# Softmax over 4096 rows of 32768: every second tile loaded in two transfers, the last tile cut finer

## The chip, the cores and the metric

The kernel runs on one core of a Trainium2 chip. The metric is the device time of one execution in microseconds: the median of three runs. A profile of one further execution, with the trace of every instruction and DMA packet, stands beside it. Five engines matter here. VectorE (DVE) takes maxima and scales, ScalarE (ACT) takes exponentials and scales, and SyncE (SP) issues transfers; ACT issues transfers too. The transfers themselves run on 16 DMA engines.

## The reference

```python
batch, seq, vocab = 16, 256, 32768
logits = np.random.randn(batch, seq, vocab).astype(np.float32)   # temperature = 1.0

scaled = logits / temperature
scaled = scaled - scaled.max(axis=-1, keepdims=True)
exp_scaled = np.exp(scaled)
return (exp_scaled / exp_scaled.sum(axis=-1, keepdims=True)).astype(np.float32)
```

A softmax over the last axis, in float32: 4096 rows of 32768 elements, 536.87 MB read and 536.87 MB written.

## The kernel before

Each row is split in two halves (`_SPLIT = 2`), so that the work is 8192 half rows of `W` = 16384 elements, 64 KB each. A tile is 128 half rows, one per partition; there are `G` = 64 tiles, and a tile's buffer takes 64 KB per partition. There are three buffers (`_BUFS = 3`), `x0` to `x2` (the trace calls all of them `x`); tile `t` uses buffer `t % 3`, is loaded into it, normalised in place and stored from it. The order of the instructions is written out by hand (`tc.manual_schedule()`); waits between engines and transfers are put in by the framework.

`normalise(t)` cuts the tile into pieces along the free axis, 4096, 4096, 4096, 2048 and 2048 elements in most tiles (`_PIECES`). It works as follows.

- For each piece, DVE takes the negated maximum `nm` of the piece (L101), and ACT replaces the piece by the exponential with that maximum as its bias, summing it into `ssum` (L108). Each piece so has its own maximum.
- The least of the negated maxima, `nMh`, is taken over the pieces (L119) and over the two halves of a row, by a shuffle between neighbouring partitions (`combine`, L77 and L80). ACT takes `ee`, the correction of each piece (L121).
- DVE sums the corrected sums (L124), combines the halves, takes the reciprocal `rS` (L135) and the final factor `f` of each piece (L136).
- Each piece is multiplied by its factor. Part of it is scaled by DVE (L140), the rest by ACT (L144); `_ON_DVE` = (4096, 4096, 2048, 0, 0) says how many elements of each piece go to DVE.

The first and the last tile, 0 and 63, are cut into four pieces of 4096 (`_END`), with 2560 elements of each on DVE (`_END_ON_DVE`). They are also loaded in four transfers of 16 KB per partition each, where other tiles are loaded in one transfer of 64 KB per partition (`_LOAD`), that is 8.39 MB. The last tile is stored piece by piece as pieces are scaled; the others in one transfer.

All loads are issued from SP (L62). Stores are issued from ACT (L70), those of the last two tiles from SP. The order is: loads of tiles 0, 1 and 2, and then for each tile `normalise(t)` and the load of tile `t + 2`, which waits until the store of tile `t - 1`, in the same buffer, has landed:

```python
for t in range(_BUFS):
    load(t)
for t in range(G):
    normalise(t)
    if t and t + _BUFS - 1 < G:
        load(t + _BUFS - 1)
```

In the trace, the load queue of SP is q1 and the store queue of ACT is q10; a transfer becomes packets of one row of one partition, so that a load of 64 KB per partition is 128 packets, eight on each DMA engine, and a four-byte completion packet on each.

Of the kernel before, what the change touches and what calls it, by code (L numbers as in the profile page):

```python
# [1 line left out]

# [4 lines left out]


_SPLIT = 2
_BUFS = 3  # L10
_LOAD = 16384
_PIECES = (4096, 4096, 4096, 2048, 2048)
_ON_DVE = (4096, 4096, 2048, 0, 0)
_END = 4096
_END_ON_DVE = 2560
_SETS = 3


@with_exitstack
def kernel(  # L20
    ctx: ExitStack,
    tc: tile.TileContext,
    logits: bass.AP,
    temperature: bass.AP,
    out: bass.AP,
):
    nc = tc.nc
    inv_t = 1.0 / float(temperature)
    P = nc.NUM_PARTITIONS
    fp32 = mybir.dt.float32  # L30
    Exp = mybir.ActivationFunctionType.Exp
    Copy = mybir.ActivationFunctionType.Copy
    X = mybir.AxisListType.X
    A = mybir.AluOpType

    xf = logits.flatten_outer_dims()
    of = out.flatten_outer_dims()
    N, V = xf.shape
    W = V // _SPLIT
    assert sum(_PIECES) == W and len(_PIECES) == len(_ON_DVE)  # L40
    x = xf.rearrange("n (h v) -> (n h) v", h=_SPLIT)
    o = of.rearrange("n (h v) -> (n h) v", h=_SPLIT)
    G = N * _SPLIT // P
    assert G * P == N * _SPLIT
    n_rounds = _SPLIT.bit_length() - 1
    K = max(len(_PIECES), W // _END)

    pool = ctx.enter_context(tc.tile_pool(name="fixed", bufs=1))
    buf = [pool.tile([P, W], fp32, tag=f"x{b}", name=f"x{b}") for b in range(_BUFS)]
    widths = dict(nm=K, ssum=K, ee=K, f=K, ttj=K, nMh=2, Sh=2, rS=1)  # L50
    stat = [
        {
            k: pool.tile([P, w], fp32, tag=f"{k}{s}", name=f"{k}{s}")
            for k, w in widths.items()
        }
        for s in range(_SETS)
    ]

    def load(t: int) -> None:
        n = _END if t in (0, G - 1) else _LOAD  # L60
        for s in range(0, W, n):
            nc.sync.dma_start(  # L62
                out=buf[t % _BUFS][:, s : s + n],
                in_=x[t * P : (t + 1) * P, s : s + n],
            )

    def store(t: int, a: int, b: int) -> None:

        engine = nc.sync if t >= G - 2 else nc.scalar
        engine.dma_start(  # L70
            out=o[t * P : (t + 1) * P, a:b], in_=buf[t % _BUFS][:, a:b]
        )

    def combine(v, op) -> None:
        for j in range(n_rounds):
            mask = [i ^ (1 << j) for i in range(32)]
            nc.vector.stream_shuffle(  # L77
                out=v[:, j + 1 : j + 2], in_=v[:, j : j + 1], mask=mask
            )
            nc.vector.tensor_tensor(  # L80
                out=v[:, j + 1 : j + 2],
                in0=v[:, j : j + 1],
                in1=v[:, j + 1 : j + 2],
                op=op,
            )

    def normalise(t: int) -> None:
        xs = buf[t % _BUFS]
        if t in (0, G - 1):
            sizes = [_END] * (W // _END)  # L90
            on_dve = [_END_ON_DVE] * len(sizes)
        else:
            sizes, on_dve = _PIECES, _ON_DVE
        K = len(sizes)
        at = [sum(sizes[:k]) for k in range(K)]
        st = stat[t % _SETS]
        nm, ssum, ee, f, ttj = (st[k][:, :K] for k in ("nm", "ssum", "ee", "f", "ttj"))
        nMh, Sh, rS = st["nMh"], st["Sh"], st["rS"]
        for k in range(K):
            xc = xs[:, at[k] : at[k] + sizes[k]]  # L100
            nc.vector.tensor_reduce(  # L101
                out=nm[:, k : k + 1], in_=xc, axis=X, op=A.max, negate=True
            )
            if inv_t != 1.0:
                nc.vector.tensor_scalar_mul(
                    out=nm[:, k : k + 1], in0=nm[:, k : k + 1], scalar1=inv_t
                )
            nc.scalar.activation(  # L108
                out=xc,
                in_=xc,  # L110
                func=Exp,
                bias=nm[:, k : k + 1],
                scale=inv_t,
                accum_out=ssum[:, k : k + 1],
            )
            if t == 1 and k == 0:

                store(0, 0, W)
        nc.vector.tensor_reduce(out=nMh[:, 0:1], in_=nm, axis=X, op=A.min)  # L119
        combine(nMh, A.min)  # L120
        nc.scalar.activation(  # L121
            out=ee, in_=nm, func=Exp, bias=nMh[:, n_rounds : n_rounds + 1], scale=-1.0
        )
        nc.vector.tensor_tensor_reduce(  # L124
            out=ttj,
            in0=ee,
            in1=ssum,
            scale=1.0,
            scalar=0.0,
            op0=A.mult,  # L130
            op1=A.add,
            accum_out=Sh[:, 0:1],
        )
        combine(Sh, A.add)
        nc.vector.reciprocal(out=rS, in_=Sh[:, n_rounds : n_rounds + 1])  # L135
        nc.vector.tensor_scalar_mul(out=f, in0=ee, scalar1=rS)  # L136
        for k in range(K):
            a, b, c = at[k], at[k] + on_dve[k], at[k] + sizes[k]
            if b > a:
                nc.vector.tensor_scalar_mul(  # L140
                    out=xs[:, a:b], in0=xs[:, a:b], scalar1=f[:, k : k + 1]
                )
            if c > b:
                nc.scalar.activation(  # L144
                    out=xs[:, b:c], in_=xs[:, b:c], func=Copy, scale=f[:, k : k + 1]
                )
            if t == G - 1:
                store(t, a, c)
        if 0 < t < G - 1:
            store(t, 0, W)  # L150

    with tc.manual_schedule():
# [8 lines that stand above are left out]
# [1 line left out]
_INS = ['logits', 'temperature']  # L162
_OUTS = [((16, 256, 32768), 'float32')]

_NUMBERS = {'temperature': 1.0}


# [26 lines left out]
```

## Time and profile before

| what | value |
|---|---|
| time, median of 3 | 2494.04 us (2493.56 to 2495.87) |
| span of the profiled execution | 2496.7 us |
| DVE busy | 1575.6 us, 63% |
| ACT busy | 1367.8 us, 55% |
| read and written | 536.87 MB each, 430 GB/s over the span |
| DVE waiting for loads (L101) | 683.8 us in 66 waits |
| ACT waiting for maxima (L108) | 1025.3 us |
| maximum of 4096 / 2048 elements, DVE | 4.413 / 2.276 us each |
| exponential of 4096 / 2048 elements, ACT | 3.708 / 1.985 us each |
| issue of a load on SP | 0.328 us (median) |

The times of DVE and ACT are sums over the whole run; what they waited for is named by the instruction that was held up. A DMA share of 1.00 in a stretch means that all 16 engines had packets in hand for all of it; values of 1.01 or a little more come from packets that began in the stretch and ended after it.

### The profile page before, as it was taken

To read this page: it belongs to the slowest core of one execution; us is meant where nothing else is said; L and a number is where in the kernel's file an instruction comes from. 1 tells how busy PE (TensorE), PEld (TensorE's weight loads), DVE (VectorE), ACT (ScalarE), POOL (GpSimd) and SP (SyncE) were. 2 spreads that over 40 slices of the span, in tenths; PEclk is the share of its full clock that TensorE was granted. 3 is DMA by queue.
4 is the path that set the end of the run, shared out by engine and by line. 5 is a ranking of instruction groups with operands and counts; after the bars stand their busy time and mean duration, and the time that the engine had idled before them with its cause. 6 is when DMAs were issued, how large, how long until landed. Compare 5 with 4: busy or idle time off the path is not lost.

```text
span 2496.7 us, 2616 instructions
## 1 busy us (share of the span) xinstructions
DVE 1575.6 (63%) x1216; ACT 1367.8 (55%) x895; POOL 0.2 (0%) x4
## 2 busy tenths in 40 slices
DVE  6576665766657656576565665656657566565665
ACT  6464654645546455464554645546455464554655
POOL 0000000000000000000000000000000000000000
DMA  9999999999999999999999999999999999999998
GB/s 419 436 429 430 433 437 436 435 437 426 434 434 437 433 426 435 434 436 423 433 433 433 435 425 436 436 433 425 435 422 436 421 437 436 421 436 422 436 429 380
DMA packets 19748, 1073.91 MB, mean 430 GB/s; under 512 B 2192, under 2 KB 2192, under 8 KB 2192
## 3 DMA queue, kind: packets, MB, share of 16 engines
q1 hardware_dynamic: 10800, 553.65, 51.4%
q10 hardware_dynamic: 8928, 520.10, 48.4%
q14 instruction: 20, 0.16, 0.0%
HBM read 536.87 MB, written 536.87 MB: 430 GB/s over the span
## 4 chain that ended last, share of the span: by engine, by line
DMA 73%; DVE 16%; ACT 9%; another core or an unknown queue 2%; issue 0%; SPq 0%; DVEq 0%; ACTq 0%
DMA x<-in_logits_dram 37%; DMA out_dram<-x 36%; DVE nm L101 12%; ACT x L108 7%; DVE x L140 3%; ACT x L144 2%; DVE f L136 0%; ACT ee L121 0%; DVE rS L135 0%; DVE Sh L80 0%; DVE ttj L124 0%; DVE Sh L77 0%; SPq L62 0%; DVEq L189 0%
## 5 line engine op out<-in xcount | busy, mean ns | idle before, releaser
L101 DVE TENSOR_REDUCE nm<-x 128x1 f32<-128x4096 f32 x318 | 1117.5, 3579 | 683.8 <-DMA x<-in_logits_dram 683.8
L108 ACT ACTIVATE x<-x,nm 128x4096 f32<-128x4096 f32 x318 | 965.4, 3036 | 1025.3 <-DVE nm L101 1025.3
L144 ACT ACTIVATE x<-x,f 128x2048 f32<-128x2048 f32 (+1 forms) x194 | 370.9, 1975 | 74.0 <-DVE f L136 74.0
L140 DVE TENSOR_SCALAR x<-x,f 128x4096 f32<-128x4096 f32 (+2 forms) x194 | 372.2, 1975 | 2.5 <-DVE f L136 0.2
L124 DVE CUSTOM_DVE_ANT_0 ttj<-ee,ssum 128x5 f32<-128x5 f32 (+1 forms) x64 | 10.6, 166 | 196.7 <-ACT ee L121 196.7
L108 ACT ACTIVATION_READ_ACCUMULATOR x<-x,nm 128x1 f32 x318 | 59.2, 186 | 0.0
L121 ACT ACTIVATE ee<-nm,nMh 128x5 f32<-128x5 f32 (+1 forms) x64 | 18.1, 284 | 0.0
L136 DVE TENSOR_SCALAR f<-ee,rS 128x5 f32<-128x5 f32 (+1 forms) x64 | 14.8, 231 | 2.2
L135 DVE RECIPROCAL rS<-Sh 128x1 f32<-128x1 f32 x64 | 10.5, 164 | 2.2
L80 DVE TENSOR_TENSOR Sh<-Sh 128x1 f32<-128x1 f32 x64 | 10.2, 159 | 2.2
L80 DVE TENSOR_TENSOR nMh<-nMh 128x1 f32<-128x1 f32 x64 | 10.2, 159 | 2.2
L119 DVE TENSOR_REDUCE nMh<-nm 128x1 f32<-128x5 f32 (+1 forms) x64 | 10.1, 158 | 2.2
L77 DVE STREAM_SHUFFLE Sh<-Sh 128x1 f32<-128x1 f32 x64 | 9.7, 151 | 0.0
L77 DVE STREAM_SHUFFLE nMh<-nMh 128x1 f32<-128x1 f32 x64 | 9.7, 151 | 0.0
L108 ACT ACT_TABLE_LOAD x1 | 1.3, 1283 | 8.1 <-DMA x<-in_logits_dram 8.1
L124 DVE DVE_READ_ACCUMULATOR2_ANT Sh<- 128x1 f32 x64 | 5.2, 82 | 0.0
L77 DVE LOAD_MASK_SELECT Sh<-Sh x64 | 0.9, 14 | 2.8
L77 DVE LOAD_MASK_SELECT nMh<-nMh x64 | 0.9, 14 | 2.8
L175 POOL MEMSET const-uint8-127<- 128x1 uint8 x1 | 0.1, 102 | 0.0
L175 POOL MEMSET const-bfloat16-1.0<- 128x1 bf16 x1 | 0.1, 101 | 0.0
L175 POOL MEMSET const-float32-0.0<- 128x1 f32 x1 | 0.1, 98 | 0.2 <-issue 0.2
L175 POOL MEMSET const-float32-1.0<- 128x1 f32 x1 | 0.1, 98 | 0.0
## 6 DMA issues: line engine op xcount, KB each, us to landing
x<-in_logits_dram SPq DMA_DIRECT2D x8, 2048.0 KB, 23.7
out_dram<-x SPq DMA_DIRECT2D x4, 2048.0 KB, 15.1
x<-in_logits_dram SPq DMA_DIRECT2D x62, 43.7
out_dram<-x ACTq DMA_DIRECT2D x62, 44.5
out_dram<-x SPq DMA_DIRECT2D x1, 29.4
```

Of the source, the lines that this page charges most:

```text
L77: nc.vector.stream_shuffle(out=v[:, j + 1 : j + 2], in_=v[:, j : j + 1], mask=mask)
L80: nc.vector.tensor_tensor(out=v[:, j + 1 : j + 2], in0=v[:, j : j + 1], in1=v[:, j + 1 : j + 2], op=op,)
L101: nc.vector.tensor_reduce(out=nm[:, k : k + 1], in_=xc, axis=X, op=A.max, negate=True)
L108: nc.scalar.activation(out=xc, in_=xc, func=Exp, bias=nm[:, k : k + 1], scale=inv_t, accum_out=ssum[:, k : k + 1],)
L119: nc.vector.tensor_reduce(out=nMh[:, 0:1], in_=nm, axis=X, op=A.min)
L121: nc.scalar.activation(out=ee, in_=nm, func=Exp, bias=nMh[:, n_rounds : n_rounds + 1], scale=-1.0)
L124: nc.vector.tensor_tensor_reduce(out=ttj, in0=ee, in1=ssum, scale=1.0, scalar=0.0, op0=A.mult, op1=A.add, accum_out=Sh[:, 0:1],)
L135: nc.vector.reciprocal(out=rS, in_=Sh[:, n_rounds : n_rounds + 1])
L136: nc.vector.tensor_scalar_mul(out=f, in0=ee, scalar1=rS)
L140: nc.vector.tensor_scalar_mul(out=xs[:, a:b], in0=xs[:, a:b], scalar1=f[:, k : k + 1])
L144: nc.scalar.activation(out=xs[:, b:c], in_=xs[:, b:c], func=Copy, scale=f[:, k : k + 1])
L175: nc = _bacc.Bacc("TRN2", target_bir_lowering=False, num_devices=1)
```

## The change

Three things are changed. An even tile other than tile 0 is loaded in two transfers, of 12288 and 4096 elements (48 and 16 KB per partition), issued one right after the other; odd tiles keep one transfer of 64 KB. The pieces are as before, so that the first three, of 4096, need only the first transfer, and the last two, of 2048, the second. The last tile is cut like the tiles in the middle, 4096 three times and 2048 twice, with another division between DVE and ACT, and is loaded and stored in those five pieces. Tile 0 stays as it was, under other names. The purpose is that the work on a tile can start before all of it has landed, and that the last stores are smaller.

```diff
-_LOAD = 16384
+_LOADS = ((12288, 4096), (16384,))
 _PIECES = (4096, 4096, 4096, 2048, 2048)
 _ON_DVE = (4096, 4096, 2048, 0, 0)
-_END = 4096
-_END_ON_DVE = 2560
+_FIRST_PIECES = (4096, 4096, 4096, 4096)
+_FIRST_ON_DVE = (2560, 2560, 2560, 2560)
+_LAST_PIECES = (4096, 4096, 4096, 2048, 2048)
+_LAST_ON_DVE = (2560, 2560, 2560, 2048, 0)
...
+    def cut(t: int) -> tuple:
+        if t == 0:
+            return _FIRST_PIECES, _FIRST_ON_DVE, _FIRST_PIECES
+        if t == G - 1:
+            return _LAST_PIECES, _LAST_ON_DVE, _LAST_PIECES
+        return _PIECES, _ON_DVE, _LOADS[t % 2]
+
     def load(t: int) -> None:
-        n = _END if t in (0, G - 1) else _LOAD
-        for s in range(0, W, n):
+        s = 0
+        for n in cut(t)[2]:
             nc.sync.dma_start(
                 out=buf[t % _BUFS][:, s : s + n],
                 in_=x[t * P : (t + 1) * P, s : s + n],
             )
+            s += n
...
     def normalise(t: int) -> None:
         xs = buf[t % _BUFS]
-        if t in (0, G - 1):
-            sizes = [_END] * (W // _END)
-            on_dve = [_END_ON_DVE] * len(sizes)
-        else:
-            sizes, on_dve = _PIECES, _ON_DVE
+        sizes, on_dve, _ = cut(t)
```

More of the change, by code (lines that the diff above doesn't have):

```diff
@@ L45 @@
     n_rounds = _SPLIT.bit_length() - 1
-    K = max(len(_PIECES), W // _END)
+    K = max(len(_FIRST_PIECES), len(_PIECES), len(_LAST_PIECES))
     pool = ctx.enter_context(tc.tile_pool(name="fixed", bufs=1))
```

## The prediction

> **What bounds the kernel now.** I read four views: the page's parts 1 to 3 (what is full), the chain of waits (what a tile is made of), stretches of 116.69 us (one round of the three buffers) beside stretches of the end, and the timeline of the last tile. From the page:
>
> ```profile
> span 2496.7 us, 2616 instructions
> DVE 1575.6 (63%) x1216; ACT 1367.8 (55%) x895; POOL 0.2 (0%) x4
> DMA  9999999999999999999999999999999999999998
> DMA packets 19748, 1073.91 MB, mean 430 GB/s; under 512 B 2192, under 2 KB 2192, under 8 KB 2192
> q1 hardware_dynamic: 10800, 553.65, 51.4%
> q10 hardware_dynamic: 8928, 520.10, 48.4%
> x<-in_logits_dram SPq DMA_DIRECT2D x62, 43.7
> out_dram<-x ACTq DMA_DIRECT2D x62, 44.5
> ```
>
> The two queues' packets fill 51.4% + 48.4% = 99.8% of the 16 DMA engines' time, while DVE has 37% and ACT 45% free. The chain of waits repeats this round, over and over:
>
> ```profile
> 274.25 44.19 DMA x<-in_logits_dram
> 318.45 13.08 DVE nm L101 x3
> 331.56 7.77 ACT x L108 x6
> ...
> 340.61 3.95 DVE x L140 x2
> 344.57 1.90 ACT x L144
> 346.50 44.52 DMA out_dram<-x
> ```
>
> Load 44.2, compute 28 and store 44.5 us make 116.7 us for one buffer. The reader must not take this as a latency bound: a tile moves 8.39 MB in and 8.39 MB out, and alone, at the full rate, each would take about 19.4 us, not 44. A transfer takes 44 us because two or three share the engines. Three buffers give one tile in 38.9 us, and the stretches say what that is:
>
> ```profile
> 158.00:2375.11 2217.11, 1402.99 (x1083) 1217.01 (x798) 0.00 (x0) 1.00 1.00 432
> 2375.10:2496.70 121.60, 73.82 (x57) 64.06 (x41) 0.00 (x0) 1.00 0.94 402
> ```
>
> (Columns: stretch, length, DVE, ACT and POOL busy, clock, DMA share, GB/s.) In the body the DMA share is 1.00 at 432 GB/s; only the end, at 0.94, has a hole:
>
> ```profile
> 2451.00:2468.00 17.00, 13.44 (x7) 15.39 (x9) 0.00 (x0) 1.00 1.01 438
> 2468.00:2471.50 3.50, 3.12 (x9) 2.36 (x2) 0.00 (x0) 1.00 0.13 56
> 2471.50:2476.00 4.50, 3.70 (x3) 3.62 (x3) 0.00 (x0) 1.00 0.96 402
> ```
>
> The store of tile 62 is out near 2469.5 and the first store of tile 63 starts near 2471.7.
>
> The packet records behind the third part give the unit prices, one packet being one partition's row: 64 KB 2.418 us, 16 KB 0.611 us, the 4-byte completion 0.009 us. Packets of the load queue and of the store queue alternate one for one when both have work. 16000 x 2.418 and 1536 x 0.611 us over 16 engines are 2476.7 us. Three things stand on top: 64 KB packets stretched past 2.418 us (13.4 us per engine; 8.2 of it in stores, 5.1 in loads); the hole of some 2.1 us at the end; and instruction fetches (20 packets of 8 KB in the span, about 0.309 us each). At the end 15 engines are done at 2491.4 to 2491.7, one at 2495.06; I read that one as the engine that carries the fetches, since 20 x 0.309 = 6.2 us less the hole of 2.1 us that it doesn't have is 4.1, near the 3.5 us it is late. That engine has no hole and no pause: it sets the end.
>
> **What the Trainium skill says.** "DMA: Bandwidth & Descriptors", section "Where 436 GB/s comes from", gives 435 GB/s as the ceiling of the fabric; the body's 432 is 0.7% under it, so the trace agrees and hardly anything is left. The same page, "Queues, rings and completion order", says that each engine goes round robin over its queues by packets; the alternation in the records agrees, with one row of up to 64 KB as the packet. Its "Rules for kernel authors" ask for at least 1 MiB per transfer; the new pieces have 6.3 and 2.1 MB, and the 2 MB transfers of tiles 0 and 63 run at 0.611 us per 16 KB, 1% off the rate of the large ones.
>
> **The change part by part.**
>
> *Loads of even tiles 2 to 62 (31 of them) in 48 and 16 KB.* Bytes stay. From the two sizes, a packet costs (2.418 - 0.611) / 48 = 0.03765 us per KB, and on top 0.611 - 16 x 0.03765 = 0.0087 us. So 48 KB costs 1.816 and the pair 2.427, against 2.418. Per tile and engine: 8 more packets x 0.0087 + one completion of 0.009 = 0.079 us; times 31 = 2.4 us. Records of 16 KB have a mean of 0.620 against the median of 0.611; with the mean, 8 x 0.0175 + 0.009 = 0.149 us, times 31 = 4.6 us. I take 2.4 and keep 4.6 as the upper end. All of it lies on the path, as nothing hides beside full engines. SP's 31 further issues (0.328 us each) run while the queue still has work.
>
> *What it moves.* DVE may start a tile on its first three pieces, and needs only 15 us after the 16 KB part instead of 28. But this shortens the tile, not the engines' work. One for one, a 48 KB packet faces a 64 KB store packet, and a 16 KB packet faces 64 KB: loads get 3/7 and then 1/5. Walk it with 19.3 us of packets for a whole transfer, 14.5 and 4.9 for the parts. At 0 an even tile's store is issued, and 4.2 us are left of the odd load in flight. Sharing evenly, the odd tile lands at 8.5; the store, with 15.1 left, then gets 4/7 beside the next even tile's first part and ends at 35. The first part ends alone at 38. The odd tile, computed in 28.4, is stored from 37, beside the second part's eight packets: 8 x (2.418 + 0.611) = 24, so both end at 62. The next odd load then runs alone, until the even tile is computed at 62 + 15.3 = 77.4; it has 4.2 us left, and the round closes: two tiles in 2 x 38.7. So stores get faster (25 and 35 us), loads slower (about 51 us whole; 54 and 78 us in parts), and the load queue always has a load waiting behind the one in flight. Nothing is gained or lost by it if the engines stay full.
>
> *Waits.* The first load of a pair waits for the buffer's store, as now; behind it on SP are only the second part and later loads, which wait for later stores. On DVE the wait for the 16 KB part stands before piece 3; behind it are the rest of this tile and the next tile, which by the walk lands 10 us and more after that. DVE's idle time per pair of tiles stays 21 us (now 10.6 a tile). So no wait is put on the path.
>
> *Tile 63 in five pieces.* From first maximum to `ee` four pieces took 21.13 us (2446.58 to 2467.71), five in tile 62 20.79 (2418.69 to 2439.48): 0.34 us earlier for the first store, inside the hole, which the engine with the fetches doesn't have. Smaller packets and one more transfer each way cost some 0.1 us; the later pieces, ready every 1.5 us, queue behind stores of 4.8 us. Tile 0 is as it was. 33 more issues and their waits may add a fetch or half of one: 0.3 us. Sum: +2.4 + 0.1 + 0.3 = +2.8 us, less at most 1 us at the end for 15 engines that don't set it: 2494.04 + 2.8 = 2496.8.
>
> **The rivals.**
>
> *Faster.* The stretched store packets are the cause that could go: most of their 8.2 us falls late in the run, about 2 us after a store is issued, on some 14 engines at once, when the load queue had just run dry (packets starting 2254.95 to 2255.6 took 2.96 to 3.50 us). The walk's standing load would end that. If the late engine counts on these too, -8.2 - 2.1 + 2.8 gives 2486.5. Against it: that engine was busy through these pauses, so they may only be the others waiting for it.
>
> *Slower by price.* The added transfers may each be stretched as loads are now, 5.1 / 63 = 0.08 us, so 31 x 0.08 = 2.5, and the 16 KB packets cost the mean: 4.6 + 0.4 + 2.5 = +7.5, 2501.5. [...]Against: the second part is queued right behind the first.
>
> *Slower by holes.* If the walk is wrong and loads run dry, each pause costs what a fresh transfer takes to start (issued 2253.07, first packet 2254.95: 1.9 us); in one of four split tiles that is 8 x 1.9 = 15 us, 2512. The depth of the load queue speaks against it.
>
> **How the numbers follow.** Forecast 57%, faster 20%, slower by price 17%, by holes 6%. The predicted time is 2496.8. The bounds of 0.2% are 2489.05 and 2499.03. Part of the faster rival would stop short of 2489, some of the forecast's own spread passes 2499: faster 0.19, same 0.57, slower 0.24. The range reaches from halfway into the faster case, 2488, to just past the price case, 2502.
>
> **What would show it.** Right: DMA share 1.00 at 431 or 432 GB/s in the body; stores landing in some 25 to 35 us, whole loads in about 50, 31 second parts far later than first parts; DVE's total wait for loads still near 680 us; the end of tile 63 still a store chain. Wrong: a body above 433 GB/s (the pauses counted), or below 430 (price or holes, the latter with slices of lower DMA share); stores still at 44 us would say that the shares by packet are not as I walk them.

## The result, and the profile after

The changed kernel takes 2628.79 us (median of 4 runs, 2602.36 to 2642.53) beside 2494.36 us for the kernel before: a ratio of 1.0503, 95% interval 1.0426 to 1.0579 (the ratio leaves out the highest of the four runs, which counts as a slow one). It is 5% slower, where 2496.8 was forecast and a range up to 2502.

From the page of the changed kernel, its busy times, its rate in 40 slices, its queues and its transfers (last column: median us from issue to landing):

```profile
span 2626.0 us, 2720 instructions
DVE 1577.9 (60%) x1217; ACT 1374.5 (52%) x897; POOL 0.2 (0%) x4
DMA  9999999999999999999999999999999999999998
GB/s 415 430 431 438 390 406 420 425 416 431 422 403 398 413 400 416 399 400 413 401 412 405 402 405 407 410 411 411 396 400 420 392 411 406 415 399 415 400 414 356
q1 hardware_dynamic: 15552, 553.66, 51.6%
q10 hardware_dynamic: 8928, 520.10, 46.9%
...
x<-in_logits_dram SPq DMA_DIRECT2D x31, 6144.0 KB, 45.8
x<-in_logits_dram SPq DMA_DIRECT2D x38, 2048.0 KB, 72.8
...
out_dram<-x ACTq DMA_DIRECT2D x62, 39.6
x<-in_logits_dram SPq DMA_DIRECT2D x31, 52.6
```

DVE and ACT do the same work as before (1577.9 and 1374.5 us, against 1575.6 and 1367.8). Bytes are the same. What is lost is the rate: the first four slices of 65.65 us (after the start-up in the first) run at 430 to 438 GB/s, near the 432 of the whole body before; from the fifth on only one does. The digits of the DMA row say 9 nearly throughout. The stretches of the changed kernel (columns: stretch, length, DVE, ACT, POOL busy, clock, DMA share, GB/s), the body first, then about two tiles in the middle:

```profile
158.00:2375.11 2217.11, 1333.48 (x1029) 1160.25 (x758) 0.00 (x0) 1.00 0.99 410
```

```profile
1505.00:1512.00 7.00, 2.40 (x2) 2.44 (x2) 0.00 (x0) 1.00 1.09 358
1512.00:1540.00 28.00, 19.30 (x17) 15.99 (x12) 0.00 (x0) 1.00 1.01 436
1540.00:1548.00 8.00, 5.32 (x3) 5.36 (x3) 0.00 (x0) 1.00 0.87 372
1548.00:1554.00 6.00, 5.23 (x2) 0.78 (x1) 0.00 (x0) 1.00 1.10 355
1554.00:1590.00 36.00, 19.27 (x18) 20.55 (x14) 0.00 (x0) 1.00 1.00 419
1505.00:1590.00 85.00, 51.53 (x40) 45.12 (x30) 0.00 (x0) 1.00 1.00 411
```

and the same 85 us of the kernel before:

```profile
1505.00:1590.00 85.00, 55.91 (x48) 48.99 (x34) 0.00 (x0) 1.00 1.00 432
```

Two things can be seen. In the body the share is still 0.99 but the rate has gone from 432 to 410 GB/s: engines with a packet in hand move fewer bytes. And the loss is not even. Between 1512 and 1540 the full rate is there, 436; in 1505 to 1512 and in 1548 to 1554 it is 355 to 358 at a share above 1, and between 1540 and 1548 engines stand idle, 0.87.

The packet records show what happens at these places. Until 1512.4 only loads are in flight (the store was issued at 1507.5); when its first packets come, 48 KB packets of the load take 2.9 to 3.5 us in place of 1.815 on 15 engines; the sixteenth, still busy with the load before, takes 4.1 us in place of 2.418 for one of 64 KB. By 1546.5 fifteen engines have emptied both queues, while one still finishes its part of a store (it is done with it at 1546.58, the others at 1541.95 to 1543.1). The next load waits for that last part and goes out at 1547.0; then store packets take 2.7 to 3.3 us, some 4.1, in place of 2.418. In the whole run packets last 104 us per engine longer than the median of their size, and 77 us of that lie in the first 10 us after the issue of a store, which are 25% of the span.

The chain of waits of the changed kernel, two consecutive tiles (start, us, what):

```profile
1006.33 46.26 DMA x<-in_logits_dram
...
1052.61 13.07 DVE nm L107 x3
1065.69 14.42 another core or an unknown queue
...
1080.13 4.49 DVE nm L107 x2
...
1093.83 10.02 another core or an unknown queue
...
1103.88 13.08 DVE nm L107 x3
...
1131.93 39.90 DMA out_dram<-x
```

The three first pieces take 13 us, and then DVE stands for 14.4 us before the last two: the 16 KB part has not landed. The chain doesn't name what released it; the timeline of a later tile does, in the same place (start, us, instruction, idle time before it and releaser):

```profile
1576.50 4.48 DVE L107 TENSOR_REDUCE nm<-x 128x1 f32<-128x2048 f32 x2 [14.66 <-DMA x<-in_logits_dram]
```

Each transfer has 16 completion packets, one per engine, and lands with the last of them. Counted from the issue, the medians of tiles 1 to 62 are (us; *middle* is the median of the 16 completions; the 72.8 us of the page are over 38 transfers, seven of them of tiles 0 and 63):

```
transfers            number   middle   15th   last
first part, 48 KB      31      31.2    33.9   45.8
second part, 16 KB     31      42.8    43.5   73.3
whole load             31      40.7    41.9   52.6
store                  62      37.0    38.5   39.6
```

So the 16 KB part has come in on fifteen engines 43.5 us after its issue, and the tile is complete only 30 us later, when a single engine is done; that is what DVE waits for. In the tile of the stretch above this engine still has packets of the first part when the others are done with both, and its second part then runs beside the next store. Which engine it is, and why it is behind, the records do not say. The early start is there, but it is given back. From the waits:

```profile
DVE nm L107 <- DMA x<-in_logits_dram: 850.8, 90, 26.7
```

DVE waits 850.8 us for loads, in 90 waits, where it waited 683.8 in 66. From factor to factor (L142), tiles that took 38.8 us each now take 37.7 and 45 in turn in the later part of the run.

### The profile page after: what moved, and what is told of

It reads as the page before. It is cut to its first block, busy times and chain, and to the rows that moved or that the text cites. A ratio compares the mean times of both kernels' runs of the same rounds, so it can differ in the third digit from the quotient of the medians.

```text
span 2626.0 us, 2720 instructions
## 1 busy us (share of the span) xinstructions
DVE 1577.9 (60%) x1217; ACT 1374.5 (52%) x897; POOL 0.2 (0%) x4
## 4 chain that ended last, share of the span: by engine, by line
DMA 46%; DVE 27%; another core or an unknown queue 16%; ACT 10%; issue 1%; SPq 0%; ACTq 0%
DMA x<-in_logits_dram 25%; DVE nm L107 21%; DMA out_dram<-x 20%; ACT x L114 7%; DVE x L146 5%; ACT x L150 3%; DVE f L142 0%; ACT ee L127 0%; DVE Sh L90 0%; DVE rS L141 0%; DVE ttj L130 0%; DVE Sh L87 0%; SPq L71 0%; ACTq L195 0%
## 5 line engine op out<-in xcount | busy, mean ns | idle before, releaser
L107 DVE TENSOR_REDUCE nm<-x 128x1 f32<-128x4096 f32 x319 | 1120.1, 3570 | 850.9 <-DMA x<-in_logits_dram 850.8
L142 DVE TENSOR_SCALAR f<-ee,rS 128x5 f32<-128x5 f32 (+1 forms) x64 | 14.8, 231 | 2.2
## 6 DMA issues: line engine op xcount, KB each, us to landing
x<-in_logits_dram SPq DMA_DIRECT2D x31, 6144.0 KB, 45.8
x<-in_logits_dram SPq DMA_DIRECT2D x38, 2048.0 KB, 72.8
out_dram<-x ACTq DMA_DIRECT2D x62, 39.6
x<-in_logits_dram SPq DMA_DIRECT2D x31, 52.6
```

What stands on the lines that cost most here:

```text
L107: nc.vector.tensor_reduce(out=nm[:, k : k + 1], in_=xc, axis=X, op=A.max, negate=True)
```

## The experiments

All times are medians of 2 to 14 runs and stand, as a ratio with its 95% interval, beside runs of the kernel before on the same chip. The edits are to the changed kernel unless said otherwise. I first asked which part of the change costs.

**The last tile alone: `last_only`.**

```diff
-_LOADS = ((12288, 4096), (16384,))
+_LOADS = ((16384,), (16384,))
```

> All loads of the middle tiles whole again, only the last tile cut in five. The theory of shares (the 48 and 16 KB packets beside 64 KB packets break the overlap of loads and stores) and that of an early start (the first three pieces begin before the tile is complete) both put the whole loss in the split: 2492 to 2496 us. If the last tile had a part in it, this kernel would lie above 2505.

Measured: 2496.62 us, ratio 1.0006 [0.9991, 1.0021]. The five pieces of the last tile cost nothing that can be measured.

**The split alone: `split_only`.**

```diff
-_LAST_PIECES = (4096, 4096, 4096, 2048, 2048)
-_LAST_ON_DVE = (2560, 2560, 2560, 2048, 0)
+_LAST_PIECES = (4096, 4096, 4096, 4096)
+_LAST_ON_DVE = (2560, 2560, 2560, 2560)
```

> The split of every second load alone, the last tile as before. Shares and early start: 2600 to 2640 us, as with the whole change. If the loss needed both parts: under 2560.

Measured: 2639.58 us, 1.0577 [1.0538, 1.0616]. The loads in two parts are the whole loss.

**The split without the early start: `late_start`.** Even tiles take the last two pieces first, so nothing starts before the 16 KB part is there.

```diff
-        for k in range(K):
+        order = (3, 4, 0, 1, 2) if 0 < t < G - 1 and t % 2 == 0 else range(K)
+        for k in order:
```

> Transfers as in the changed kernel, but in the even tiles DVE and ACT take the pieces of the 16 KB part first, so that no work on a tile starts before nearly all of it has landed, as with whole loads. Shares: the loss stays, 2580 to 2660 us, since the packets are the same. Early start: the loss goes, under 2520 us.

Measured: 2593.9 us, 1.0394 [1.0361, 1.0427]. Most of the loss, 3.9% of 5.0%, is there without the early start, so that part lies in the transfers.

**Every load in two parts: `all_split`.**

```diff
-_LOADS = ((12288, 4096), (16384,))
+_LOADS = ((12288, 4096), (12288, 4096))
```

> Every load of tiles 1 to 62 in 48 and 16 KB. A price per transfer or per packet would double the loss, to some 2750 us. Shares: the loss stays or shrinks, 2500 to 2640, since all tiles are alike again, but 16 KB packets still face 64 KB ones. If it is the unlikeness of neighbouring tiles alone that costs, it comes near 2500.

Measured: 2642.37 us, 1.0588 [1.0566, 1.0611]. Twice the added transfers and hardly more loss: it is not a price per transfer.

**Equal halves: `halves_loads`, `halves_both`.** The first cuts every load into two of 32 KB per partition, the second the stores as well (the lines from `_STORES` on belong to it alone). The last tile is as in the kernel before in these, in `halves_early` and in all following experiments with `_STORES`.

```diff
-_LOADS = ((12288, 4096), (16384,))
+_LOADS = ((8192, 8192), (8192, 8192))
+_STORES = ((8192, 8192), (8192, 8192))
...
-            store(t, 0, W)
+            s = 0
+            for n in _STORES[t % 2]:
+                store(t, s, s + n)
+                s += n
```

> Loads of tiles 1 to 62 in two transfers of 32 KB per partition, stores whole, the last tile as before. Shares: packets of 32 KB face stores of 64 KB, so loads get a third where both have work; the loss stays, 2540 to 2660 us. If only the small 16 KB part is harmful (it gets a fifth): 2500 to 2520, the price of the packets (about 0.08 us a tile) and little more.

> As halves_loads, but the stores too go in two transfers of 32 KB per partition, so that packets of both queues are of one size. Shares: the loss goes, 2494 + 62 x 0.16 = 2504 us, between 2495 and 2515. A loss that comes from cutting loads in two, from the early start or from the number of transfers: above 2540.

Measured: `halves_loads` 2606.19 us, 1.0444 [1.0422, 1.0466]; `halves_both` 2494.19 us, 0.9993 [0.9985, 1.0002]. With 32 KB packets in both queues the loss is gone, though there are four times as many added transfers as in the change. The body of `halves_both` has the full rate:

```profile
158.00:2375.11 2217.11, 1408.47 (x1083) 1217.89 (x800) 0.00 (x0) 1.00 1.00 433
```

**The unlike packets on the other side: `mirror`** (loads whole, stores of even tiles in 48 and 16 KB: `_LOADS = ((16384,), (16384,))`, `_STORES = ((12288, 4096), (16384,))`).

> Loads whole, the stores of the even tiles in 48 and 16 KB instead. Shares: unlike packets again, now in favour of the loads; slower by 1% or more, 2520 to 2650 us. Early start and anything that belongs to loads alone: 2494 to 2500.

Measured: 2504.45 us, 1.0034 [1.0013, 1.0054]. About a tenth of the loss of the change or less, which fits neither of the two expected ranges: that packets are unlike is not enough, and which queue has the smaller ones matters.

**The engine that was last: `more_fetch`.** In the kernel before, GpSimd gets idle work, so that more instructions are fetched.

```diff
+            nc.gpsimd.tensor_copy(out=spare, in_=stat[t % _SETS]["rS"])
+            for _ in range(40):
+                nc.gpsimd.memset(spare, 0.0)
```

> The kernel before, with 41 further tiny instructions per tile on the idle GpSimd, 2624 in all, which wait for the tile's reciprocal and write a spare column[...]. If the engine that carries the fetches sets the end, as I predicted, 20 x 0.3 to 20 x 0.7: 2500 to 2508 us. If it does not set the end: 2492 to 2498.

Measured: 2494.42 us, 0.9999 [0.999, 1.0008], with 42 fetch packets in place of 20. By my reading of the last engine, 22 packets of 0.309 us should have cost 6.8 us. They cost nothing, so that reading is not supported. Nor does one engine fall behind: from 1500 us on the last completion of a transfer comes 0.6 us after the last but one, where it was 4.6 us in the kernel before.

**The same two sizes in both queues: `matched`** (every load and every store in 48 and 16 KB).

> Loads and stores of all tiles 1 to 62 in 48 and 16 KB, so that both queues carry the same unlike packets. If it is the unlikeness between the queues that costs, the loss of the all-split kernel (2642 us) goes: 2494 to 2515 us. If a 16 KB part behind a 48 KB part is bad in itself: above 2540.

Measured: 2689.75 us, 1.0792 [1.0744, 1.0839], the slowest of all, which I had not expected. Its stretches, by quarters of the span:

```profile
0.00:670.00 670.00, 422.80 (x324) 367.53 (x238) 0.20 (x4) 1.00 1.00 431
670.00:1340.00 670.00, 391.67 (x304) 342.93 (x224) 0.00 (x0) 1.00 0.97 400
1340.00:2010.00 670.00, 387.14 (x294) 332.94 (x217) 0.00 (x0) 1.00 0.94 391
2010.00:2690.00 680.00, 376.23 (x295) 328.71 (x217) 0.00 (x0) 1.00 0.90 375
```

For 670 us nothing is lost, and then the share itself falls to 0.90. The completion records show what grows: a transfer has landed when the last of the 16 engines has written its completion. In the first 300 us that is 1.5 us after the median of the engines, from 1200 to 2400 us 33 to 35 us after it, and from 1500 to 2400 us nearly all of that (30 to 34 us) is one engine. Between 300 and 1200 us, where the lag grows to 25 us, the last two engines are on average within 1.5 us of each other, so more than one is late there. So engines drift behind, in the end one alone, and a buffer that is stored is not free before the last of them is done.

**Stores begun early: `halves_early`** (`halves_both` with each half stored as soon as it is scaled).

> As the kernel with halves in both directions (2494 us), but the first half of a tile is stored as soon as it is scaled, some 4 us before the second. The queues are never dry there, so earlier stores can't gain in the body: 2488 to 2498 us, the gain, if any, at the end.

Measured: 2494.1 us, 0.9991 [0.9983, 1.0]. No gain beyond the noise: with engines at 433 GB/s hardly anything is left to gain by starting earlier.

**What a fresh queue costs: `sparse` and `dense`.** Only transfers: 64 loads and 20 stores of 64 KB per partition; the stores are spaced by idle ACT work in `sparse` and queued back to back in `dense`; loads into two buffers, stores from one that never changes. All computation is left out.

```diff
-_SPACE = 66
+_SPACE = 0
```

> A kernel that leaves the computation out: 64 whole loads that nothing reads, one after the other, and 20 whole stores of a zero tile, one every 75 us or so, spaced by dummy activations, so that each store starts while loads alone are running. 84 x 8.39 MB at 432 GB/s are 1631 us. If the restart of a dry store queue costs the 1 to 2 us per engine that the records show around it: 20 to 40 us more than the dense kernel. If a restart costs nothing: within 5 us of it.

> The same 64 loads and 20 stores without the dummy activations: the stores run back to back beside the loads, with up to four waiting, so that their queue is dry only once, after the last. Restart theory: 1630 to 1640 us, and 20 to 40 us less than the sparse kernel. Without it: the same as the sparse kernel.

Measured: `sparse` 1695.47 us, `dense` 1640.26 us. This shows no price of a start: of the 55 us, some 45 are idle engines at the end of `sparse`, whose last store starts late. Packets that last longer than the median of their size differ by 16.8 us per engine (19.4 against 2.6), but of the 19.4 only 2.6 lie in the first 5 us after the issue of a store and 4.0 in the first 10, so a store that begins beside running loads costs next to nothing here, some 0.2 us. In the changed kernel it is 77 of 104. `dense` shows, too, that loads alone for some 835 us lose next to nothing (430 GB/s, against 434 with stores beside them).

**Drift against steady loss: `sync_before`, `sync_after`, `sync_matched`.** Two one-column writes on DVE after every sixth tile make the next load wait until the store of that tile has landed, so that all engines stand level ten times in a run. I put them into the kernel before, the changed one and `matched`.

```diff
+            if t % 6 == 5 and t + _BUFS < G:
+                nc.vector.memset(buf[t % _BUFS][:, 0:1], 0.0)
+                nc.vector.memset(buf[(t + 2) % _BUFS][:, 0:1], 0.0)
```

> The kernel before, with two one-column memsets by DVE after every sixth tile (in columns that are already stored or about to be loaded), so that the next load waits until the store just issued has landed on all 16 engines: the engines start the next six tiles in step. Ten such stops; this run gives their price, for which I reckon 3 to 5 us each: 2525 to 2545 us.

> The changed kernel with the same stops. If the loss comes from engines that drift apart (one falls further and further behind, the rest wait for it), the stops cut it before it has grown, and the time falls to near that of the kernel before with stops: 2525 to 2560 us. If it comes from the unlike shares alone, which form again within a tile or two: no gain, 2625 to 2680 us.

> The kernel with 48 and 16 KB parts in both queues (2690 us) with the same stops. Drift: 2530 to 2570 us. No drift: 2680 us or more.

Measured: 2539.48 us, 1.0176 [1.0142, 1.0209]; 2624.94 us, 1.0518 [1.0459, 1.0577]; 2547.52 us, 1.0208 [1.0134, 1.0283]. The stops themselves cost 44 us. With them `matched` is 8 us above `sync_before`, where it was 195 above the kernel before: its loss grows over many tiles and goes when the engines are brought level, as drift would have it. (A stop also empties both queues, so that loads and stores meet in a fresh order; no run separates the two. And `matched` itself ran on another chip.) The changed kernel is still 85 us above, of 134: the lag of the last engine behind the median falls from 10.3 to 3.1 us on average, but most of the loss stays. It is back between any two stops, where six tiles take 246 us against 238 in `sync_before`. In the first 140 us after a stop both move 427 GB/s on average; in the next 60 us it is 387 against 435.

**Whose packets are smaller, and is one size always free: `halves_stores`, `quarters_both`** (loads whole with stores in 32 KB halves; loads and stores all in 16 KB quarters).

> Loads whole, every store in two transfers of 32 KB per partition: halves_loads turned round. Theory A as I have it now (loads with the smaller packets lose their share, the store queue runs dry and the queues take turns alone; the other way round the loads go ahead, a load is waiting for its buffer, and the stores queue stays full): near the time before, 2494 to 2510, with stores landing slower than 45 us and loads faster than 43, and the load queue, not the store queue, dry for part of the time. Theory B (unlike packets cost the same whichever queue has the smaller): as halves_loads, some 2600.

> Every load and every store of tiles 1 to 62 in four transfers of 16 KB per partition, stores after the whole tile is scaled. Theory A (what costs is packets of unlike size in flight together, wherever they come from; one size everywhere costs only the price per packet): one size again, so no loss beyond the price: 24 more packets of load and 24 of store per tile and engine at 0.0087 us, 62 tiles, 26 us if none of it is hidden, 2494 to 2520, stretched packets and lag as before; halves_both had a fifth of this priced at 10 us and showed nothing, so I expect 2494 to 2505. Theory B (splitting transfers costs by their number, halves_both was lucky): twice as many transfers as matched or more, 2600 and above.

Measured: `halves_stores` 2495.01 us, 0.9997 [0.9986, 1.0007]; `quarters_both` 2504.45 us, 1.003 [1.002, 1.0039]. One size everywhere stays nearly free, even at six added transfers a tile. And the same two sizes, 64 against 32 KB, cost 4.4% when the loads have the smaller packets and nothing when the stores have. The transfers and the body of `halves_loads`:

```profile
x<-in_logits_dram SPq DMA_DIRECT2D x124, 4096.0 KB, 51.2
...
out_dram<-x ACTq DMA_DIRECT2D x62, 35.1
```

```profile
158.00:2375.11 2217.11, 1337.69 (x1029) 1159.68 (x761) 0.00 (x0) 1.00 0.98 413
```

and of `halves_stores`:

```profile
out_dram<-x ACTq DMA_DIRECT2D x122, 4096.0 KB, 40.8
...
x<-in_logits_dram SPq DMA_DIRECT2D x62, 33.6
```

```profile
158.00:2375.11 2217.11, 1405.86 (x1085) 1218.88 (x799) 0.00 (x0) 1.00 1.00 432
```

In both, the queue with the 64 KB packets is served faster (35.1 and 33.6 us, against about 44 before). What follows differs. With fast stores, tiles come in bunches: their periods (from factor to factor) go, for instance, 27.9, 66.2, 27.9, 46.7, 30.0, 62.2 us, where 27.9 is the computation alone, a tile that had been waiting for DVE. With fast loads the periods stay between 37.5 and 40.5 us after the first two tiles, apart from the last. Bunches alone are not the loss, though: in `mirror` periods of 31 to 34 and of 45 to 47 us alternate nearly throughout.

**The sum.** From the packet records, per engine: *stretched* is time of packets beyond the median of their size (excesses under 0.02 us left out), *idle* is time without a packet between the first and the last, *price* is the added packets at 0.0087 us and completions at 0.009. A queue is counted as empty where at most three of its data packets fall into 5 us on all 16 engines together, the start and the end of the run left out. *Lag* is the mean of the last engine's completion behind the median one, over loads and stores.

```
kernel         span     stretched  idle   price   empty: loads  stores   lag
before         2496.7    14.1       0.8    -          59          41      5.5
after          2626.0   104.2      38.0   2.5         52         284     10.3
split_only     2645.1   102.5      59.0   2.4         39         295     12.3
late_start     2597.9    56.0      57.9   2.5        161         545     10.2
all_split      2638.1    79.5      72.4   5.0         90         599     20.6
halves_loads   2606.3    68.8      51.6   4.9        126         542     15.3
matched        2692.2    78.5     121.4   9.7        372         372     22.5
mirror         2501.4    15.1       2.9   2.4        239           9      6.1
halves_stores  2492.7     9.8      -2.9   4.8        395           0      3.8
halves_both    2491.9     2.2      -1.3   9.7          0           0      4.0
```

(Idle comes out slightly negative where packets overlap on an engine by a little.) For the changed kernel, 90.1 us of stretched packets, 37.2 of idle time and 2.5 of price over the kernel before are 129.8; the spans differ by 129.3. The sum closes as well for `all_split` (65.4 + 71.6 + 5.0 = 142.0 against 141.4), `halves_loads` (110.4 against 109.6) and `matched` (194.7 against 195.5). That it closes proves no cause: on an engine the packets and the gaps between them make up the span, so it must. What it says is where the time is. In the changed kernel two thirds are packets that last longer than their size explains, and most of the rest is engines without a packet; in `matched` it is one third and nearly two thirds.

What decides whether it occurs is less settled. Shown is which edit brings the loss and which removes it: smaller packets in the loads alone bring it, one size in both queues or the smaller ones in the stores do not. In the table the lossy kernels have the store queue empty for 284 us and more, the others for 41 at most, while the load queue may be empty for 395 us without harm (`halves_stores`). That is a parallel and no proof: in `dense` the store queue is empty for 835 us at hardly any loss, and in `sparse` its starts cost next to nothing. What the stores of the changed kernel meet when they start, and those of `sparse` do not, was not tried. Why packets are stretched on all engines at once, and which engine drifts and why, stays open. The lag is not the whole of it: with stops the lag of the changed kernel's loads falls from 15.1 to 3.2 us, and 85 of 134 us stay.

## Why the prediction was wrong

- *The engines are the bound, at 432 GB/s.* Right for the kernel before, and it is why nothing was to be gained: `halves_early`, where loads are halved and the first half of a tile is stored early, is at 0.9991.
- *The price per packet, +2.4 us.* The right order, and too small to matter here. `halves_both` has four times that price and is no slower: its stretched packets fall from 14.1 to 2.2 us. That was the term of the rival "faster", and it was real, but it went with 32 KB packets in both queues, not with the change, under which it grew to 104.2. In `quarters_both` the priced packets (some 29 us) overestimate the cost, 8.5 us.
- *The shares by packet.* Right in direction, and where the numbers meet it is by luck. Stores got faster, but only to 39.6 us in the median, outside the 25 and 35 of the walk. Whole loads took 52.6 us (51 in the walk), first parts 45.8 (54) and second parts 73.3 (78); but fifteen of the 16 engines had them in after 41.9, 33.9 and 43.5 us, and the rest is one engine. On the fifteen the second part does not run beside a store for 24 us, as in the walk: it is done some 10 us after the first. "Queues, rings and completion order" in the Trainium skill's "DMA: Bandwidth & Descriptors" (each engine alternates between its queues by packets) explains the direction, and `halves_loads` and `halves_stores` agree with it from both sides.
- *"Nothing is gained or lost by it if the engines stay full", and "the load queue always has a load waiting behind the one in flight".* This is the step that failed: what the engines lose when the queues take turns was put at nothing. The walk itself has stores absent from 35 to 37 and from 62 to 77.4 us of a pair, some 540 us in 31 pairs, and I let that pass, since one queue can fill the engines (`dense`). Measured, the store queue is empty for less, 284 us, and yet each engine loses 90.1 us to stretched packets and 37.2 us to gaps; two tiles take 83 us in the later part of the run, for 77.4. The walk also took the 16 engines as one, all in step. They are not: loads land 15.1 us after their median engine on average and stores 3.2, and DVE's waits before the last two pieces are waits for one engine. How much of the loss comes from that, and how much from packets stretched on all engines, stays open.
- *The rival "slower by holes".* Right in direction, at 6%, and far too small. It has loads run dry, but the load queue is empty for 52 us, no longer than before (59); it is the store queue that runs dry, and two thirds of the loss are no holes at all. It priced a pause of 1.9 us in one of four split tiles; measured are 129.3 us over 31 pairs, 4.2 us in each. What "speaks against it", the depth of the load queue, was an output of the walk that it should have tested.
- *The last engine carries the fetches and sets the end.* Not supported (`more_fetch`). That it was late at the end was the visible part of the drift: already in the kernel before the lag grows from 1.5 us in the first 300 us to some 7.5 between 1500 and 2400. It was read as a feature of the end, where it was a sign of engines out of step.
- *No wait on the path.* DVE's wait was to stay near 680 us; it is 850.8. The order of its waits was as told, but the wait for the 16 KB part, put at no cost, is one for the slowest engine (14.66 us in the tile shown).
- *The last tile, nothing.* Right: `last_only` at 1.0006 [0.9991, 1.0021].
- *The signs.* "Below 430 (price or holes, the latter with slices of lower DMA share)": the body is at 410, with a share of 0.99. Two thirds of the loss show in no share of busy time at all, only in bytes per second. The sign "31 second parts far later than first parts" came true, for the reason above and not for the walk's.

## What to carry to other kernels

Where loads and stores together fill the DMA engines, as in this kernel, try one packet size in both, or leave the smaller ones to the stores: packets of 32 and 64 KB cost 4.4% one way round and nothing the other, 32 KB in both nothing, and a mixture of 48 and 16 KB in both, 7.9%, the most of all. Before splitting a transfer for an earlier start, ask whether the computation is what the buffers wait for; with the engines at their rate there is nothing to win, and the order in which buffers come free is at stake. In such a kernel read the rate beside the busy share, and look at how far the last engine's completion lies behind the others'.

## What was not expected of the hardware

- Engines of one transfer drift apart. In `matched` one engine fell 34 us behind the median; with ten stops the lag was 4.4 us on average, and 1.0792 became 1.0208, the stops included. In the changed kernel fifteen engines had a second part after 43.5 us and the last after 73.3. In `halves_both` the lag also grows, to 7.2 us, without any loss; by the count above neither queue is ever empty there.
- A packet can take far longer than its size: 48 KB 2.9 to 3.5 us for 1.815, on 15 engines at once, when the other queue started, and 64 KB 4.1 for 2.418 on the sixteenth. In the kernel before such time was 14.1 us in all, with 32 KB packets on both sides 2.2.
- Size alone does not give the rate. "Rules for kernel authors" in the Trainium skill's "DMA: Bandwidth & Descriptors" asks for 1 MiB per transfer; the parts here have 2.1 and 6.3 MB, and 5% was lost beside transfers of 8.4 MB. The same 2.1 MB on both sides (`quarters_both`) lose 0.3%.
